# Queries, keys, the convolution's inputs and all gates as pairs of seven block products, with two of four weight sums made by accumulating transfers

## The chip, the cores and the metric

The kernel runs on one core of a Trainium2 chip. The metric is the device time of one execution in microseconds. TensorE multiplies matrices, VectorE and ScalarE work on tiles, GpSimd (POOL) and SyncE (SP) mostly issue transfers. Each engine runs its own instructions in the order in which they stand in the program and waits on semaphores for the others.

## What is computed

One step of a trunk with two layers, for 512 frames of a new stream (the prompt) and 8 x 16 frames of running streams (the sample), 640 rows together, in float32. All widths are multiples of 128; D_MODEL is 1024.

```python
for l in range(2):
    x = x + 0.5 * swiglu(rmsnorm(x), w_ffn1_gu[l], w_ffn1_down[l])
    h = rmsnorm(x)
    B, C, V, q, k, v, g = split(h @ w_in[l])        # 512 each, g: 2 x 1024
    g_conv, g_attn = split(sigmoid(g + b_gate[l]))
    y_conv = B * depthwise_conv3(C * V)             # new_conv: last two rows of C * V
    y_attn = softmax(q k^T / 8 + bias, banded) v    # 8 heads x 64; sample: cached keys, values
    m = g_conv * (y_conv @ w_conv_out[l]) + g_attn * (y_attn @ w_attn_out[l])
    x = x + m @ w_o[l]
    x = x + 0.5 * swiglu(rmsnorm(x), w_ffn2_gu[l], w_ffn2_down[l])
y = rmsnorm(x)                                      # also returned: k, v, new_conv of both layers
```

## The kernel before

**Layout and precision.** Everything is kept transposed: a tile has 128 features in its partitions and the 640 rows along it. Each float32 operand is split into a high and a low part (`whi`, `wlo` for weights, `hhi`, `hlo` for h), and a product is the sum of three matmuls: high with high, high with low, low with high. A projection to 128 columns is 8 tiles x 3 x 2 halves of 320 rows, 48 matmuls.

**Weights.** `wst` is one stream of slabs of 128 x 1024 in the order of use. `load` brings a slab into one of three `raw` buffers (issued by SP), `prep` casts it to its high part on ScalarE (L248), `flush` subtracts that for the low part on VectorE (L253). There are three buffers of each part; `slab` keeps two slabs prepared ahead of the one in use.

**Pairs by seven products.** The FFN's gate and up projections, and gates 4 to 15 of the mixer, are computed two at a time by seven products of half size instead of eight (a scheme of Strassen's kind). Their seven left factors are weight blocks and sums of weight blocks, their right factors halves of h and differences of such halves. `source` makes four weight sums for each pair on VectorE. One block product is 12 matmuls of 320 columns (`block`, L331). Three PSUM tiles pa, pb, pc take them in turn, and between the products parts are copied out by ScalarE (c1, u2, c5) and added by VectorE.

**A layer** is FFN, mixer, FFN. In the mixer the order on TensorE is: q and k of the first head pair, V for all rows (L1051), and then attention, with `fill(n)` between its steps; `fill` takes the next n steps (8 weight tiles make a projection's 8 steps of 6 matmuls each) of a stream of projections: q and k of the other head pairs, then for each of four column groups C, V and B of the convolution, then two gates. For each head pair p, `scores(p)` multiplies queries with keys for both heads (L1089; reductions with bias L1091), `softmax` takes exponentials on ScalarE (L1221) and scales on VectorE (L1225), `values(p)` transposes (L1111), copies (L1113) and multiplies with v (L1124). Then the eight sample streams follow: `sscores(b)` (L1160) and `svalues(b)` (L1175 to L1193). After that come gates 2 and 3, the first output products (`out`, 24 matmuls each), the pairs of gates with two output products each, and w_o.

**Who orders what.** In the FFNs and from gate 2 on TensorE, VectorE and ScalarE run in the order of the code. In the attention only TensorE's order is the code's; the framework's scheduler places the instructions of VectorE, ScalarE, POOL and SP.

**PSUM.** The eight banks are two double tiles `acc` (projections; scores of the widest tile) and four single tiles `att`. A projection alternates between the two `acc` tiles, and VectorE scales it out with the rows' norm `rr` (L422, L1012).

Of the kernel before, what the change touches and what calls it, by code (L numbers as in the profile page):

```python
# [10 lines left out]
F32 = mybir.dt.float32  # L11
# [32 lines left out]
GP = 4  # L44

# [35 lines left out]
def mixer_order():  # L81


    out = [("g", m) for m in range(GP)] + [("co", m) for m in range(GP)]
    for b, name in enumerate(("co", "ao")):
        for m in range(0 if b else GP, KT, 2):
            out += [("gu", b * KT + m), (name, m), (name, m + 1)]
    return out + [("o", m) for m in range(KT)]


def kinds():
# [23 lines left out]
    for l in range(L):  # L115
        ffn(f"a{l}")
        held = KT * (3 * CT + 3 * AW // P)
        for what, _ in mixer_order():
            if what == "gu":
                plain(held)  # L120
                held = 0
                out.append("mix")
            else:
                held += KT if what in ("g", "o") else CT
        plain(held)
        ffn(f"b{l}")
# [12 lines left out]
def trunk(ctx: ExitStack, tc: tile.TileContext, xin, wst, small, pbias, samplebias, kcache, vcache,  # L139
# [10 lines left out]
    ps2 = ctx.enter_context(tc.tile_pool(name="ps2", bufs=2, space=PSUM))  # L150
    ps1 = ctx.enter_context(tc.tile_pool(name="ps1", bufs=4, space=PSUM))
# [3 lines left out]
    def acc(name):  # L155
        return ps2.tile([P, 2, 512], F32, tag="acc", name=name)

    def att(name):
        return ps1.tile([P, 512], F32, tag="att", name=name)
# [21 lines left out]
    sums, pool = {}, [None]  # L181
# [16 lines left out]
    def source(i):  # L198
# [3 lines left out]
        if i not in sources:  # L202
# [4 lines left out]
            elif arg == 0:  # L207
                sources[i] = [(ra, whole)]
            else:
# [148 lines left out]
    def norm(name, goff, ssum):  # L358
# [21 lines left out]
        def sums():  # L380
            st.sums([ssum], att(f"nps{name}"))
            st.roots()
            st.turn(ssum, st.r)

        def spread():
            for a in range(2):
                c = slice(a * HT, (a + 1) * HT)
                ps = att(f"nbc{name}_{a}")[:, :HT]
# [254 lines left out]

    def gate_up(fp, n, ex, first, turned, tails, put, j):
# [160 lines left out]
    def mixer(l, after):  # L805
        with tc.tile_pool(name=f"yp{l}", bufs=1, reuse_waits="tile") as yp:
# [4 lines left out]
            ycs = [yp.tile([P, T], F32, name=f"yc{l}_{c}") for c in range(CT)]  # L811
            with tc.tile_pool(name=f"mp{l}", bufs=2, reuse_waits="tile") as mp:
                cn = mp.tile([P, CT, 2 * (1 + NB)], F32, name=f"cn{l}", bufs=1)
                gates = {}

                def gate(m, then=None):
                    for _ in gate_steps(m, then):
                        pass

                def gate_steps(m, then=None):  # L820
                    pg = acc(f"pgate{l}_{m}")
                    yield from steps(pg, h)
                    if then:
                        then()
                    gates[m] = tmp(f"g{l}_{m}")
                    scaled(gates[m], pg, rr)
                    sigmoid(gates[m], m)

                def sigmoid(g, m, scale=1.0):
                    bg = O_BG + l * 2 * KT + m  # L830
                    ACT.activation(g, g, AF.Sigmoid, bias=sm[:, bg : bg + 1], scale=scale)

                def others():
                    for c in range(CT):
                        yield from conv(l, c, h, rr, cn, ycs[c])
                    POOL.dma_start(co[l], cn)
                    for m in range(2):
                        yield from gate_steps(m)

                with tc.manual_schedule(engines={mybir.EngineType.PE}):  # L840
                    attention(l, h, st, stats, mp, yas, others())
            with tc.tile_pool(name=f"gp{l}", bufs=1, reuse_waits="tile") as gp, \
                 tc.manual_schedule(engines=ORDERED):
                hold[0] = True
                mo = outputs(l, gp, h, st, ycs, yas, gate, sigmoid, gates)
# [13 lines left out]
    def outputs(l, gp, h, st, ycs, yas, gate, sigmoid, gates):  # L859
# [6 lines left out]
        ts = [tuple(gp.tile([P, 4, HT], F32R, name=f"t{i}{l}_{kp}") for i in ("hi", "lo"))  # L866
              for kp in range(NP)]

        A, B = (0, 1), (2, 3)

        def operands(kp, two):

            z = spare[kp % 2].rearrange("p a (b t) -> p (a b) t", b=2)
            (xe, ge), (xo, go) = ((x[k], O_GM + l * KT + k) for k in (2 * kp, 2 * kp + 1))
            ge, no, go = sm[:, ge : ge + 1], less[:, go - O_GM : go - O_GM + 1], sm[:, go : go + 1]
            if two is A:
                ACT.activation(z[:, 3], xe[:, t2], AF.Copy, scale=ge)
            for o, a, s, b in (((1, xe[:, t1], ge, 3), (0, xo[:, t2], no, 1)) if two is A else
                               ((2, xo[:, t2], go, 3), (3, xo[:, t1], no, 0))):
                DVE.scalar_tensor_tensor(out=z[:, o], in0=a, scalar=s, in1=z[:, b],  # L880
                                         op0=ALU.mult, op1=ALU.subtract)
            c = slice(two[0], two[1] + 1)
            ACT.copy(ts[kp][0][:, c], z[:, c])

        def rest(kp, two):
            z = spare[kp % 2].rearrange("p a (b t) -> p (a b) t", b=2)
            c = slice(two[0], two[1] + 1)
            DVE.tensor_tensor(out=ts[kp][1][:, c], in0=z[:, c], in1=ts[kp][0][:, c].bitcast(F32),
                              op=ALU.subtract)

        def halves_of_h(odd, c):
            return lambda kp: tuple(z[:, c] for z in h[2 * kp + odd])

        def made(i):
            return lambda kp: tuple(z[:, i] for z in ts[kp])

        X11, X21, X22 = halves_of_h(0, t1), halves_of_h(1, t1), halves_of_h(1, t2)
        XN6, XT5, XT7, XT4 = (made(i) for i in range(4))
        c1, u2 = st.caps[:, t1], st.caps[:, t2]
        every = range(NP)  # L900

        def gate_pair(m, then=None):
# [3 lines left out]
            c5 = gp.tile([P, HT], F32, tag="cap", name=f"c5_{n}")  # L906
# [60 lines left out]
        gate(2, lambda: (flush(), take(yc, "yc", ycs), operands(0, A), operands(0, B)))  # L967
        flush()
        gate(3, lambda: (rest(0, A), rest(0, B), operands(1, A), operands(1, B)))
        rest(1, A)  # L970
        rest(1, B)
        operands(2, A)
        flush()
        out(0, yc)
        rest(2, A)
        operands(3, A)
        out(1, yc)
        rest(3, A)
        operands(2, B)
        out(2, yc)  # L980
        rest(2, B)
        operands(3, B)
        out(3, yc)
        rest(3, B)
        for m in range(GP, 2 * KT, 2):
# [8 lines left out]
    def attention(l, h, norms, stats, mp, yas, others):  # L994
# [13 lines left out]
        def qproj(p):  # L1008
            pq = acc(f"pq{l}_{p}")
            yield from steps(pq, h)  # L1010
            t = qa[p] = mp.tile([P, T], F32, name=f"q{l}_{p}", tag="q")
            DVE.scalar_tensor_tensor(out=halves(t), in0=two(pq), scalar=HD ** -0.5,  # L1012
# [493 lines left out]
```

## Time and profile before

| | |
|---|---|
| median of 3 runs | 2611.59 us (2611.41 to 2613.09) |
| profiled execution, its own time | 2611.54 us |
| its span | 2609.8 us |
| TensorE busy | 2591.7 us, 17864 matmul records |
| VectorE, ScalarE, POOL busy | 1831.2, 1053.3, 46.4 us |
| granted TensorE clock | full in every slice |
| HBM traffic | 90 GB/s over the span |

The page lists busy time by engine and groups of instructions by line. A matmul's record is about 0.31 us long for 320 columns, but records overlap, so that the time on the path is read from the chain of waits. PE is TensorE, DVE VectorE, ACT ScalarE. Times in the timeline and the chain are microseconds from the span's start.

### The profile page before, as it was taken

The numbers are of one execution on the slowest core, as the hardware profiler recorded it, in microseconds if no ns is written. First come the engines' busy times: TensorE is split into PE (matmuls) and PEld (weight loads), VectorE is DVE, ScalarE is ACT, GpSimd is POOL, SyncE is SP. The second block draws the span as 40 slices with busy tenths as digits, with TensorE's granted clock in tenths as the row PEclk, the third lists the DMA queues.
The fourth block names the chain that finished last, engine by engine and source line by source line (L and its number), as shares of the span: only waits on it lengthen the run. The fifth ranks groups of instructions, "written<-read, shape, count | busy, mean of one in ns | idle before, by whom it ended". The sixth has DMA issues, their size and how long they took to land.

```text
span 2609.8 us, 42561 instructions
## 1 busy us (share of the span) xinstructions
PE 2591.7 (99%) x17864; PEld 2538.0 (97%) x17864; DVE 1831.2 (70%) x2771; ACT 1053.3 (40%) x1586; POOL 46.4 (2%) x137
## 2 busy tenths in 40 slices
PE   8999999999999999999999999999999999999998
PEld 8999999889999999999999999998899999999998
DVE  7687767364777887767787667664547778867676
ACT  5343334342444443334454333343324445433332
POOL 0000000110000000000000000001100000000000
PEclk9999999999999999999999999999999999999999
DMA  3222223334222132222222222233331222222222
GB/s 131 73 105 82 73 89 116 110 104 140 67 81 89 59 112 82 73 89 81 82 81 98 75 92 77 86 116 113 112 132 65 81 81 75 90 93 75 88 90 74
DMA packets 73808, 237.06 MB, mean 91 GB/s; under 512 B 7984, under 2 KB 18864, under 8 KB 73616
## 3 DMA queue, kind: packets, MB, share of 16 engines
q1 hardware_dynamic: 70016, 223.90, 25.3%
q0 software_dynamic: 2880, 9.79, 1.0%
q8 instruction: 140, 2.29, 0.3%
q10 hardware_dynamic: 720, 0.65, 0.1%
q14 instruction: 52, 0.43, 0.1%
HBM read 225.85 MB, written 7.94 MB: 90 GB/s over the span
## 4 chain that ended last, share of the span: by engine, by line
PE 94%; DVE 4%; ACT 1%; issue 0%; DMA 0%; SPq 0%; DVEq 0%; ACTq 0%
PE pab L331 12%; PE pda L317 11%; PE pdb L317 11%; PE paa L331 11%; PE pcb L331 6%; PE pca L331 5%; PE py L317 4%; PE po L317 4%; PE qa L331 3%; PE pbb L331 3%; PE pba L331 3%; PE pc L317 2%; PE pq L317 2%; PE pb L317 2%; PE pgate L317 2%; PE pcv L317 2%
## 5 line engine op out<-in xcount | busy, mean ns | idle before, releaser
L253 DVE TENSOR_TENSOR wlo<-raw,whi 128x1024 fp32r<-128x1024 f32 (+2 forms) x492 | 530.4, 1083 | 177.1 <-ACT whi L248 177.1
L248 ACT CAST whi<-raw 128x1024 fp32r<-128x1024 f32 (+2 forms) x492 | 461.3, 940 | 349.8 <-PE pca L331 79.4
L331 PE MATMUL pab<-xhib,whi 128*128 128x320 f32 x704 | 218.4, 310 | 0.4 <-ACT u_b L728 0.4
L331 PE MATMUL pab<-xlob,whi 128*128 128x320 f32 x704 | 217.4, 309 | 0.0
L331 PE MATMUL pab<-xhib,wlo 128*128 128x320 f32 x704 | 217.4, 309 | 0.0
L331 PE MATMUL paa<-xhia,whi 128*128 128x320 f32 x640 | 198.2, 310 | 0.7 <-ACT c_a L664 0.5
L331 PE MATMUL paa<-xloa,whi 128*128 128x320 f32 x640 | 197.7, 309 | 0.0
L331 PE MATMUL paa<-xhia,wlo 128*128 128x320 f32 x640 | 197.7, 309 | 0.0
L317 PE MATMUL pda<-ahia,whi 128*128 128x320 f32 x704 | 160.4, 309 | 0.6 <-DVE x L794 0.6
L317 PE MATMUL pda<-aloa,whi 128*128 128x320 f32 x704 | 160.4, 309 | 0.0
L317 PE MATMUL pda<-ahia,wlo 128*128 128x320 f32 x704 | 160.4, 309 | 0.0
L317 PE MATMUL pdb<-alob,whi 128*128 128x320 f32 x656 | 149.5, 309 | 0.0
L317 PE MATMUL pdb<-ahib,wlo 128*128 128x320 f32 x656 | 149.4, 309 | 0.0
L317 PE MATMUL pdb<-ahib,whi 128*128 128x320 f32 x656 | 149.4, 309 | 0.0
L331 PEld LDWEIGHTS pab<-xhib,whi 128*128 128x128 f32 x704 | 132.2, 188 | 1.2 <-ACT u_b L728 0.9
L331 PEld LDWEIGHTS pab<-xlob,whi 128*128 128x128 f32 x704 | 132.2, 188 | 0.2
L331 PEld LDWEIGHTS pab<-xhib,wlo 128*128 128x128 f32 x704 | 132.2, 188 | 0.0
L331 PEld LDWEIGHTS paa<-xhia,whi 128*128 128x128 f32 x640 | 120.2, 188 | 1.3 <-ACT c_a L664 0.8
L331 PEld LDWEIGHTS paa<-xloa,whi 128*128 128x128 f32 x640 | 120.2, 188 | 0.1
L331 PEld LDWEIGHTS paa<-xhia,wlo 128*128 128x128 f32 x640 | 120.2, 188 | 0.0
L248 ACT CAST whi<-s 128x1024 fp32r<-128x1024 f32 (+1 forms) x96 | 94.3, 982 | 63.4 <-DVE s L192 51.9
L317 PEld LDWEIGHTS pda<-ahia,whi 128*128 128x128 f32 x704 | 117.6, 188 | 1.1 <-issue 1.1
(486 smaller groups left out, 6689.8 us busy)
## 6 DMA issues: line engine op xcount, KB each, us to landing
raw<-in_wst SPq DMA_DIRECT2D x384, 512.0 KB, 3.5
kc<-in_kcache SPq DMA_DIRECT2D x16, 512.0 KB, 4.3
vc<-in_vcache SPq DMA_DIRECT2D x16, 512.0 KB, 4.4
bias<-in_pbias POOLq DMA_DIRECT2D x16, 256.0 KB, 3.1
x<-in_xin SPq DMA_DIRECT2D x8, 320.0 KB, 5.2
out_ko<-k POOLq DMA_DIRECT2D x8, 320.0 KB, 2.5
out_vo<-v POOLq DMA_DIRECT2D x10, 256.0 KB, 2.6
out_yout<-x SPq DMA_DIRECT2D x8, 192.0 KB, 1.9
```

Source lines behind the costliest of these rows:

```text
L248: ACT.copy(hi[:, d], src[:, c])
L253: DVE.tensor_tensor(out=lo, in0=src, in1=hi.bitcast(F32), op=ALU.subtract)
L317: PE.matmul(ps[:, a, :HT], w, x[:, a * HT : (a + 1) * HT], start=k == 0 and j == 0, stop=k == n - 1 and j == 2)
L331: PE.matmul(ps, a, b, start=start and kp == 0 and j == 0, stop=stop and kp == NP - 1 and j == 2, skip_group_check=True)
```

## The change

The projections q, k, C, V and B (four each of 128 columns) and gates 0 to 3 are now made in pairs by `seven`: q with k of a head pair, C with V of a column group, two B, two gates. V (the values) is projected first; q and k of the first head pair follow it. The right factors (`Operands`) are made once, at the end of the FFN and during V, and serve the gates as well; one of them takes the place of a half of h after V has used it. `rr` is applied after the pair, for C times V as its square.

Of a pair's four weight sums VectorE makes two, and two are made by transfers issued on POOL that add slab halves from HBM onto the raw buffer. This holds for the mixer's pairs, also for gates 4 to 15; the FFN's keep their sums. The sum that stays apart lies in SBUF instead of PSUM.

PSUM is divided anew by `layout`: in the attention four single banks `pr` for the pairs and four `att`; elsewhere as before. The widest score tile now uses `att` too, and the order of score tiles is 0, 1, 3, 2. In SBUF the sample's keys use the buffers of q and k (two transfers of half size for each stream), its scores those of the transposed weights, its new values those of the bias, and the scratch for POOL's transfer descriptors is set to 2048.

The stream that `fill` takes has 140 steps instead of 160; the sample's `fill(6 + b % 2)` becomes `fill(4)`.

```diff
 def mixer_order():
-    out = [("g", m) for m in range(GP)] + [("co", m) for m in range(GP)]
...
+    mix = lambda *rows: ("mix", rows)
+    out = [("v", None)] + [mix(("q", p), ("k", p)) for p in range(AW // P)]
+    for c in range(0, CT, 2):
+        out += [mix(("C", c + i), ("V", c + i)) for i in range(2)] + [mix(("B", c), ("B", c + 1))]
+    gates = [mix(("g", m), ("g", m + 1)) for m in range(0, 2 * KT, 2)]
...
     def source(i):
...
             elif arg == 0:
                 sources[i] = [(ra, whole)]
+                if kind == "mix":
+                    rb = load(n + 1)
+                    POOL.dma_start(rb[:, h1], wst[n + 1][:, h2], accum_op=ALU.add)
...
                 elif arg == 1:
                     flush()
-                    st = sums[n] = att(f"s6_{n}")
-                    add(ra[:, h1], ra[:, h1], rb[:, h1])
-                    add(st, ra[:, h1], rb[:, h2])
-                    add(rb[:, h1], rb[:, h1], rb[:, h2])
+                    st = sums[n] = spool[0].tile([P, CH // 2], F32, tag="s6", name=f"s6_{n}", bufs=1)
+                    add(st, rb[:, h1], ra[:, h1])
+                    POOL.dma_start(ra[:, h1], wst[n + 1][:, h1], accum_op=ALU.add)
                     sources[i] = [(st, h1), (rb, h1)]
...
+    def seven(n, bank, X, c1, u2, c5, first, second, third, last):
+        pa, pb, pc = (bank(f"m{i}{n}")[:, :HT] for i in "abc")
+        def mul(ps, s, half, x, start):
+            for ks in (range(NP // 2), range(NP // 2, NP)):
+                block(ps, s, half, x, ks, start, True)
+                yield
+        s = chunk()
+        yield from mul(pa, s, 0, X["11"], True)
+        ACT.copy(c1, pa)
+        yield from mul(pb, s, 1, X["21"], True)
+        first(pb)
+        s = chunk()
+        yield from mul(pa, s, 0, X["N6"], False)
+        ACT.copy(u2, pa)
+        yield from mul(pc, s, 1, X["T5"], True)
+        ACT.copy(c5, pc)
+        s = chunk()
+        yield from mul(pa, s, 0, X["T7"], False)
+        second(pa)
+        yield from mul(pc, s, 1, X["22"], False)
+        third(pc)
+        s = chunk()
+        yield from mul(pa, s, 0, X["T4"], False)
+        last(pa)
...
     def mixer(l, after):
...
+                def upper(u):
+                    return lambda pb: add(u[:, t1], pb, cs[0]), lambda pc: add(u[:, t2], pc, cs[1])
+                def lower(g, scale=-1.0):
+                    def by(c, src):
+                        DVE.scalar_tensor_tensor(out=g[:, c], in0=src, scalar=scale, in1=rr[:, c],
+                                                 op0=ALU.mult, op1=ALU.mult)
+                    def second(pa):
+                        add(g[:, t2], pa, cs[2])
+                        by(t2, g[:, t2])
+                    return second, lambda pa: by(t1, pa)
...
-    def attention(l, h, norms, stats, mp, yas, others):
+    def attention(l, h, norms, stats, ops, mp, yas, both, others):
...
-            for i in (0, NQ - 1, *range(1, NQ - 1)):
+            for i in (0, 1, NQ - 1, *range(2, NQ - 1)):
                 w = (i + 1) * P
-                if i == NQ - 1:
-                    both = acc(f"pss{l}_{p}")
-                    pss = [both[:, e, :w] for e in range(2)]
-                else:
-                    pss = [att(f"pss{l}_{hh}_{i}")[:, :w] for hh in heads]
+                pss = [att(f"pss{l}_{hh}_{i}")[:, :w] for hh in heads]
...
-    def conv(l, c, h, rr, cn, y):
+    def conv(l, c, pair, upper, c5, rr2, cn, y):
...
+        def third(pc):
+            half(pc)
+            DVE.tensor_tensor(out=ct, in0=ct, in1=rr2, op=ALU.mult)
+            minus(u[:, 2 + HT : 2 + SEQ], y[:, HT:SEQ], ct[:, HT:SEQ])
+            minus(us[:, :, 2:], samp(y), samp(ct))
...
+        yield from pair(f"cv{c}", first, lambda pa: add(y[:, t2], pa, c5), third,
+                        lambda pa: minus(u[:, 2 : 2 + HT], pa, ct[:, t1]))
```

More of the change, by code (lines that the diff above doesn't have):

```diff
@@ L812, in mixer @@
+            layout(f"a{l}", 0)
             with tc.tile_pool(name=f"mp{l}", bufs=2, reuse_waits="tile") as mp:
                 cn = mp.tile([P, CT, 2 * (1 + NB)], F32, name=f"cn{l}", bufs=1)
[L814 to L827, printed above, removed]
@@ L865, in outputs @@
         mm = ycs + [spare[i // 2][:, i % 2] for i in range(CT)]
[L866 to L899, printed above, removed]
+        X11, X21, X22, XN6, XT5, XT7, XT4 = (X[i] for i in ("11", "21", "22", "N6", "T5", "T7", "T4"))
+        c1, u2, c5 = cs
         every = range(NP)
@@ L965, in give @@
                 mo.append(parts(hp, "h", f"m{l}_{m}", mm[m]))
[L967 to L985, printed above, removed]
+        gate_pair(2, lambda: take(yc, "yc", ycs))
+        for m in range(4):
+            out(m, yc)
+        for m in range(4, 2 * KT, 2):
             gate_pair(m, (lambda: take(ya, "ya", [yas[:, c, :] for c in range(CT)])) if m == KT else None)
@@ L1378, in trunk @@
     fp.close()
+    ps.close()
 def _cols(w):
```

257 lines of the change are left out of this document (163 added, 94 removed).

## The prediction

> **What bounds the kernel.** I read the page's busy line and its chain of waits first, then busy time by stage, then the chain in order of time inside the mixer.
>
> ```profile
> PE 2591.7 (99%) x17864; PEld 2538.0 (97%) x17864; DVE 1831.2 (70%) x2771; ACT 1053.3 (40%) x1586; POOL 46.4 (2%) x137
> ...
> PE 94%; DVE 4%; ACT 1%; issue 0%; DMA 0%; SPq 0%; DVEq 0%; ACTq 0%
> ```
>
> TensorE is busy for 99% of the span and carries 94% of the chain. Whatever takes matmuls away shortens the run, as long as nothing else becomes late. So the stages that change have to be read one by one.
>
> ```profile
> core 0: us, PE busy (x) PEld busy (x) DVE busy (x) ACT busy (x) POOL busy (x), PEclk, DMA share, GB/s
> 412.00:447.00 35.00, 35.00 (x241) 35.00 (x240) 25.41 (x30) 16.40 (x21) 1.56 (x5) 1.00 0.42 139
> 490.60:578.00 87.40, 87.40 (x611) 77.48 (x611) 52.42 (x151) 37.97 (x97) 12.67 (x33) 1.00 0.30 101
> 578.00:676.00 98.00, 98.00 (x846) 89.47 (x841) 41.38 (x85) 28.08 (x53) 4.04 (x19) 1.00 0.40 134
> 720.00:820.00 100.00, 100.00 (x683) 100.00 (x682) 72.25 (x104) 44.24 (x65) 0.00 (x0) 1.00 0.25 85
> ```
>
> Of these windows of layer 0, the first is the end of the FFN ahead of the mixer, the second the prompt attention (softmax of eight heads between projections), the third the sample attention, the fourth the gates. TensorE never stops in any of them. VectorE has 52.4 of 87.4 us in the prompt attention and 41.4 of 98 in the sample attention: room on average. The question is what each single wait then becomes.
>
> **The saving.** The chain gives the price of a projection and of a pair by seven block products.
>
> ```profile
> 500.23 7.04 PE pk L317 x48
> ...
> 515.29 2.36 PE pss L1089 x16
> ...
> 521.36 7.04 PE pk L317 x48
> ...
> 536.42 2.36 PE pss L1089 x16
> ...
> 717.62 7.04 PE py L317 x48
> 736.99 7.04 PE py L317 x48
> ```
>
> A projection of 48 matmuls takes 7.04 us on the path, or 0.147 us per matmul, although one record lasts 0.31 (they overlap). From 717.62 to 736.99 lie one gate pair by seven products and two output products of 24 matmuls (together 7.04): the pair costs 19.37 - 7.04 = 12.33, where two projections cost 14.08. The change makes pairs of four q with k, four C with V, two B and two of gates in each layer, 24 in all. They save 24 x 1.75 = **42.0 us**. The block products already run at this price, so nothing on TensorE itself can spoil it. Gates 4 to 15 were pairs before and keep their matmuls.
>
> **What becomes tight.** A projection had two double banks, and VectorE had 7 us to empty one. `seven` writes blocks of 12 matmuls, 1.76 us each, into three banks of a ring of four: pa, pb, pa, pc, pa, pc, pa. A bank must be read before the next block but one: three ScalarE copies (c1, u2 of pa, c5 of pc), VectorE's `second` (pa plus c5), and `last`, which frees pa for the next pair's pb. Each has 1.76 us of cover. The FFN, ordered by hand, does this with next to no wait:
>
> ```profile
> PE paa L331 <- ACT c_a L664: 0.5, 1, 0.5
> ```
>
> ```profile
> L192 DVE TENSOR_TENSOR ga<-paa,c_a x40: 484/491/493, 78.9 to 1697.2; 128x320 f32<-128x320 f32 x40
> L742 DVE TENSOR_TENSOR ga<-paa,rhoa x40: 482/484/492, 81.7 to 1700.6; 128x320 f32<-128x320 f32 x40
> L717 ACT COPY c_a<-paa x38: 406/425/428, 98.1 to 1690.1; 128x320 f32<-128x320 f32 x38
> ```
>
> An eviction needs 0.4 or 0.5 us. But in the attention only TensorE's order is written by hand; on ScalarE and VectorE the scheduler interleaves the evictions with softmax. In the order of the built program, the same in both layers, they stand behind it. The rows of before price that queue; next starts are taken from start to start.
>
> ```profile
> 515.84 0.29 DVE L1091 CUSTOM_DVE_ANT_0 s<-pss,bias 128x128 f32<-128x128 f32 x1 [4.39 <-issue]
> ...
> 517.24 0.69 DVE L1091 CUSTOM_DVE_ANT_0 s<-pss,bias 128x512 f32<-128x512 f32 x1
> ...
> 517.85 0.42 DVE L1091 CUSTOM_DVE_ANT_0 s<-pss,bias 128x256 f32<-128x256 f32 x1
> ...
> 518.54 0.55 DVE L1091 CUSTOM_DVE_ANT_0 s<-pss,bias 128x384 f32<-128x384 f32 x1
> ...
> 519.49 0.29 DVE L1219 TENSOR_SCALAR st<-st 128x4 f32<-128x4 f32 x2
> ...
> 522.17 0.79 DVE L1012 SCALAR_TENSOR_TENSOR q<-pq,rrm 128x640 f32<-128x640 f32 x1
> 522.88 1.34 DVE L1225 TENSOR_SCALAR s<-s,st 128x128 f32<-128x128 f32 x4
> ...
> 524.48 1.28 DVE L1225 TENSOR_SCALAR s<-s,st 128x128 f32<-128x128 f32 x4
> 525.67 1.22 DVE L253 TENSOR_TENSOR wlo<-raw,whi 128x1024 fp32r<-128x1024 f32 x1
> ```
>
> ```profile
> 519.75 0.40 ACT L1221 ACTIVATE s<-s,st 128x128 f32<-128x128 f32 x1 [3.81 <-DVE st L1219]
> ...
> 521.95 0.39 ACT L1221 ACTIVATE s<-s,st 128x128 f32<-128x128 f32 x1
> ...
> 524.14 1.03 ACT L248 CAST whi<-raw 128x1024 fp32r<-128x1024 f32 x1
> ```
>
> With scores at 515.3 as zero: reductions of the two heads' tiles from 0.6 to 4.2, eight exponentials from 4.4 to 8.8 (2.2 a head), each head's four scalings 1.3, the next weights' low part 1.2, high part 1.0. In the new kernel the reductions of the wide tile wait for nothing extra, but all eight score tiles share four banks, so the scores take 2.65 instead of 2.36: 0.3 each time. Then, period by period (zero at the scores' start):
>
> - Scores 0 come between blocks 2 and 3 of the second q,k pair. A half low part (0.6) sits among the reductions; exponentials run 4.3 to 8.7. The u2 copy is behind all eight, done at 9.15. TensorE has done blocks 3 and 4 at 2.65 + 3.52 = 6.17 and block 5 needs u2: 3.0. With the banks 3.3.
> - Scores 1 come after block 3. The c5 copy is behind the exponentials (3.75 to 8.15) and is ready at 8.6; TensorE stands from 6.17: 2.4. Then `second` is behind the second head's scalings (9.6) and a low part (10.8), done at 11.25, where block 6 ended at 10.36: 0.9. The next pair's first weight sum stands ahead of the reductions and waits for its transfer: 0.3 (below). With the banks 3.9.
> - Scores 2 come after block 4. A weight sum among the reductions costs 0.3 more on the banks. `last` stands behind a q eviction and both heads' scalings (11.2), a half low part and itself: 12.2; the next pair's pb wants it at 10.0. In all 2.9.
> - Scores 3 come after block 5. `last` is behind one head's scalings: 0.8. c1 of the next pair is behind the exponentials, three casts and the convolution's first tap: 1.15. With the banks 2.25.
>
> That is 12.35 a layer, **+24.7 us**. Bounds: 6 a layer, if short operations overlap more than their starts show; 17, if nine further evictions around them each meet half a cast (0.5).
>
> **Transfers.** Of a pair's four weight sums VectorE keeps two; two become accumulating transfers of 256 KB on the POOL queue, 72 in all. No accumulate is in the trace. Nearest rows:
>
> ```profile
> raw<-in_wst SPq DMA_DIRECT2D x384, 512.0 KB, 3.5
> ...
> bias<-in_pbias POOLq DMA_DIRECT2D x16, 256.0 KB, 3.1
> ```
>
> ```profile
> 519.39 1.06 POOL L1075 DMA_DIRECT2D bias<-in_pbias  x2 [10.08 <-DVE st L1091]
> ```
>
> A plain load of the same size on the same queue lands in 3.1 us, and issuing takes POOL 0.53. Below that I see no reason to go; twice it, 6.2, is the upper bound. I take 4.0, nearer the load, since reading the destination adds to the data and not to the fixed part. The Trainium skill (Collectives: The Full Stack, "The bandwidth ceiling: the fold count and why AG ≠ RS ≠ AR") says that an adding transfer is slowed by its two source reads, not by the addition. With the fit that the Trainium skill gives (DMA: Bandwidth & Descriptors, "Anatomy of one DMA — SWDGE (gpsimd) path") for twice the bytes, that is an estimate of 3.2 us; the sum by it would be 2592. No run here shows it yet.
>
> With three raw buffers the next pair's second half can be loaded only when this pair's third weight slab has been split, some 1.3 to 3 us into the pair. Add 3.5 and 4.0, and the sum can be made 9 to 11 us into the pair. The sample attention's order puts that add ahead of `second`. What the sample matmuls add there lengthens a pair:
>
> ```profile
> 585.04 0.38 PE L1175 MATMUL sptp<-ident,ss 128*128 128x128 f32 x2
> ...
> 588.10 0.67 PE L1160 MATMUL spss<-kc,bd 128*32 128x272 f32 x8
> 588.69 0.42 PE L1187 MATMUL spy<-vn,spn 16*32 16x128 f32 x8
> 589.04 0.65 PE L1187 MATMUL spy<-vc,spt 128*32 128x128 f32 x16
> ```
>
> about 2 us for each sample, nine half blocks of 0.88: a pair of fourteen lasts 15.4, and block 7 wants `second` at about 12.5. After the add come a low part and `second`, 2.1 us. In the first B pair the load is behind the sample's keys and the maximum's negation is behind the add; the exponential and c5 follow it, which costs 1.5. The other pairs come out within 0.5 and make 1.0. That is 2.5 a layer, **+5.0 us**; at 3.1 it would be about 1 for both layers, at 6.2 about 27 with what it adds in the prompt part. Each us of latency past 4.0 costs about 5 a layer. In front of the transfers POOL holds only issues, small copies and fills whose producers are done earlier; SP's loads wait for the sample's key buffers, which come free before the raw buffers do.
>
> In the gates the queue is ordered and a period is 19.37: the load starts 4.5 in, has landed and accumulated at 12.0, and the first sum is asked for at 13.9. Nothing; VectorE sheds two sums of four.
>
> **The rest.** V goes first, and the operands of the products (16 half-width tiles a layer) move from the gates into the FFN's end and V. VectorE has 25.4 of 35 us there, the change adds about 6 inside 3.5 us of slack per product: 0.5 a layer, between 0 and 2. Cover for V's evictions is the ending product. **+1.0 us**.
>
> Sum against the profiled execution's 2611.5 (span 2609.8 and 1.7 around it; the median is 2611.6): 2611.5 - 42.0 + 24.7 + 5.0 + 1.0 = **2600**. Bounds: -42 + 12 + 1 to -42 + 34 + 27 + 4, so 2582 to 2634.
>
> **Rivals.**
> *All hidden.* The FFN's pairs speak for it, VectorE's average too. Then only banks and a few tenths stay: 2575. The written order behind the exponentials speaks against it. 0.10.
> *The gain is just eaten.* If those nine evictions do meet half a cast each and the sample pairs lose 3.5 instead of 2.5, waits are 17 + 3.5 a layer, 41: 2611. 0.16.
> *Late accumulates.* They land after 6.2 us instead of 4.0. VectorE, which runs in order, stands at the add; `second`, c5 and through them blocks 6 and 7 wait in every sample pair and the scores of period 1 start their softmax late. 2600 + 2.2 x 10 = 2622, slower; it decides from about 5.2 us on. For it: the destination must be read too, and loads of keys run beside. Against: DMA engines are busy 0.40 at most. 0.22. The Trainium skill (SBUF — State Buffer, "SBUF: two separate sides" and the section on the bandwidth-pool intuition after it) has a rule of this kind: while VectorE is in a two-port mode, POOL cannot write descriptors, and a transfer of 0.62 us took 3.1. By that rule each transfer would take another 2.5 us, an estimate, and the time would be 2625. The trace does not bear it out: VectorE's scalings take 1.34 us for 1280 elements, no faster per element than its subtractions (1.22 for 1024), and POOL's two bias issues beside the reductions took their usual 1.06. It holds 0.03 of the 0.22.
> That the pairs don't save what they should is excluded by the 12.33 above.
>
> **Numbers.** The forecast near 2600 has 0.52. A measurement of this kernel tells about 0.2%, 5.2 us, from no change. Faster: 0.52 and 0.10, **0.62**; within: **0.16**; slower: **0.22**. The range leaves out 0.08 below and 0.12 above: 2586 to 2619, whose upper part is the late accumulates' shorter half. The likeliest case alone is 2590 to 2606.
>
> **What would show it.** Seven-block pairs of 12.33 without waits; TensorE waiting on the u2 copy in period 0, on c5 and `second` in period 1, on `last` in 2 and 3, about 3, 3, 2 and 2 us, twice; accumulates landing in about 4 us; no wait in the gates. TensorE's idle time should rise from 18 us to near 48. Wrong if TensorE waits for weight slabs (high or low parts), if accumulates take over 5 us, or if the scores' banks cost more than 0.5 a time.

## The result, and the profile after

The changed kernel takes 2657.76 us (median of 4 runs, 2655.37 to 2662.21) against 2611.81 (4 runs of the kernel before, 2611.41 to 2613.09): 1.0176 times as long, 95% interval 1.0160 to 1.0192. The forecast was 2600, its range ended at 2619, and the case "slower" had 0.22. The profiled execution took 2655.37 us, with a span of 2653.6.

The busy line and the accumulates' row of the DMA issues of the page after:

```profile
PE 2580.9 (97%) x17576; PEld 2513.8 (95%) x17576; DVE 1912.3 (72%) x2965; ACT 1117.7 (42%) x1738; POOL 119.2 (4%) x225
...
raw<-in_wst POOLq DMA_DIRECT2D x72, 256.0 KB, 4.1
```

The matmuls went as planned (17864 to 17576 records, 288 less: 24 pairs by 12). But TensorE's busy time fell by 10.8 us and not by 42, and its idle time (span less busy) rose from 18.1 to 72.7. So there are two losses to find: 54.6 us of new waits, and 31 us of busy time that should have gone and did not. Busy time by stage of layer 0 says where (V and the first pair; prompt attention; sample attention; gates from 4 on):

```profile
core 0: us, PE busy (x) PEld busy (x) DVE busy (x) ACT busy (x) POOL busy (x), PEclk, DMA share, GB/s
447.79:493.23 45.44, 45.44 (x244) 40.16 (x242) 28.61 (x44) 21.21 (x34) 8.04 (x13) 1.00 0.41 110
493.23:599.54 106.31, 92.78 (x593) 79.06 (x592) 72.25 (x191) 50.35 (x124) 21.61 (x42) 0.97 0.42 115
599.54:700.93 101.39, 85.26 (x722) 74.86 (x720) 61.87 (x134) 42.12 (x85) 15.80 (x34) 0.97 0.56 151
...
743.20:843.20 100.00, 99.51 (x678) 99.25 (x678) 66.31 (x94) 44.07 (x66) 7.87 (x9) 1.00 0.41 109
```

Only the two attention stages lose: 13.5 of 106 us and 16.1 of 101 us idle, and there alone the granted clock is below one (0.97). The gates have no loss worth the name. From the mixer's first product (a q before, a V now) to the first output product a layer took 243.8 us before and takes 265.6 (layer 0) and 264.6 (layer 1) now, although half of the expected saving, 21 us, lies in each. What TensorE waited for, the view of waits:

```profile
PE pss L1185 <- DVE st L1187: 13.5, 8, 2.8
PE mc_b L350 <- ACT c L682: 8.5, 2, 6.2
PE ma_cv L350 <- DVE yc L208: 6.3, 4, 2.0
...
PE qa L350 <- ACT ya L1299: 4.4, 2, 2.2
PE ma_b L350 <- ACT capsm L675: 4.3, 2, 2.3
PE mc_qk L350 <- ACT c L682: 3.5, 2, 1.9
PE ma_qk L350 <- ACT capsm L680: 3.5, 2, 2.5
PE ma_cv L350 <- ACT capsm L675: 3.4, 2, 1.7
PE spy L1289 <- DVE ss L1282: 3.1, 2, 1.6
PE ma_b L350 <- DVE sst L1320: 2.6, 2, 2.0
```

(Total us, times, longest.) The first row is the scores' banks, 13.5 us; the rows of the q,k pairs and c1 (`ma_cv` from L675) are the evictions behind softmax; the rest belongs to the sample stage, some 29 us. VectorE's own waits name what is behind them, first in the kernel before, then in the one after:

```profile
DVE s L192 <- DMA raw<-in_wst: 1.2, 4, 0.4
```

```profile
DVE s L208 <- DMA raw<-in_wst: 107.9, 38, 6.5
```

The first sum of a pair's weight blocks waited 1.2 us in all for its transfer; now VectorE stands at it for 107.9 us. What that does is seen at the worst wait, in the timelines of VectorE, ScalarE and TensorE in the first B pair:

```profile
613.96 0.08 DVE L1265 DVE_READ_ACCUMULATOR2_ANT sst<- 128x1 f32 x1
620.56 0.69 DVE L208 TENSOR_TENSOR s<-raw,raw 128x512 f32<-128x512 f32 x1 [6.52 <-DMA raw<-in_wst]
621.17 0.15 DVE L1320 TENSOR_SCALAR sst<-sst 128x1 f32<-128x1 f32 x1
...
621.41 0.52 ACT L1322 ACTIVATE ss<-ss,sst 128x272 f32<-128x272 f32 x1 [5.99 <-DVE sst L1320]
...
621.93 0.40 ACT L682 COPY c<-mc_b 128x320 f32<-128x320 f32 x1
...
622.38 0.63 PE L350 MATMUL mc_b<-hhim,whi 128*128 128x320 f32 x1 [6.20 <-ACT c L682]
```

VectorE has the sample's maximum at 614.0, but the sum of the next pair's weights stands ahead of its negation and waits until 620.56 for the accumulate. ScalarE's exponential waits for that negation, the copy c5 for the exponential, and TensorE for the copy: 6.2 us, for weights that no matmul needs yet. The chain of waits shows the same in layer 1 as a loop:

```profile
1959.72 3.55 DMA raw<-in_wst
...
1964.03 6.50 DMA raw<-in_wst
...
1971.32 1.12 DVE wlo L272
...
1979.35 3.41 DMA raw<-in_wst
...
1983.37 5.84 DMA raw<-in_wst
...
1989.23 0.70 DVE s L208
```

Load of a pair's second slab, accumulate into it, sum, and with the low part a buffer comes free for the next load: from 1959.72 to 1979.35 one round takes 19.6 us. The five rounds between 1902 and 1998 take 18.5 to 19.7 each. Four pairs of this stage (1913.9 to 1993.6) take 19.9 us each, where the same four take 15.9 in the kernel below that makes all sums on VectorE; the prediction had put 15.4.

### The profile page after: what moved, and what is told of

Read it like the earlier page. It is cut to its first block, busy times and chain, and to the rows that moved or that the text cites. A ratio compares the mean times of both kernels' runs of the same rounds, so it can differ in the third digit from the quotient of the medians.

```text
span 2653.6 us, 42700 instructions
## 1 busy us (share of the span) xinstructions
PE 2580.9 (97%) x17576; PEld 2513.8 (95%) x17576; DVE 1912.3 (72%) x2965; ACT 1117.7 (42%) x1738; POOL 119.2 (4%) x225
## 5 line engine op out<-in xcount | busy, mean ns | idle before, releaser
L272 DVE TENSOR_TENSOR wlo<-raw,whi 128x1024 fp32r<-128x1024 f32 (+2 forms) x540 | 563.0, 1047 | 183.6 <-ACT whi L267 183.1
L267 ACT CAST whi<-raw 128x1024 fp32r<-128x1024 f32 (+2 forms) x540 | 490.2, 912 | 298.1 <-PE pca L350 79.4
L267 ACT CAST whi<-s 128x1024 fp32r<-128x1024 f32 (+1 forms) x120 | 109.4, 912 | 123.0 <-DVE s L208 95.3
L272 DVE TENSOR_TENSOR wlo<-s,whi 128x1024 fp32r<-128x1024 f32 (+1 forms) x120 | 127.2, 1060 | 4.2 <-ACT whi L267 4.0
```

Of the source, the lines that this page charges most:

```text
L267: ACT.copy(hi[:, d], src[:, c])
L272: DVE.tensor_tensor(out=lo, in0=src, in1=hi.bitcast(F32), op=ALU.subtract)
```

## The experiments

Theory: late sums. VectorE stands at a weight sum (or at a low part whose high part waits) until an accumulate has landed, and reductions, negated maxima and evictions stand behind it. First rival: the queue that the prediction priced, evictions behind softmax. Second: weights are late by their loads alone.

One run of one version says little below 7 us: the four runs of the changed kernel lie between 2655.37 and 2662.21.

**Without the transfers, and with all sums on VectorE.** The first kernel leaves two of the four sums out, the second makes all four on VectorE.

```diff
-                    POOL.dma_start(rb[:, h1], wst[n + 1][:, h2], accum_op=ALU.add)
...
-                    add(st, rb[:, h1], ra[:, h1])
-                    POOL.dma_start(ra[:, h1], wst[n + 1][:, h1], accum_op=ALU.add)
+                    add(ra[:, h1], ra[:, h1], rb[:, h1])      # second kernel only; the first
+                    add(st, ra[:, h1], rb[:, h2])             # keeps add(st, rb, ra) alone
+                    add(rb[:, h1], rb[:, h1], rb[:, h2])
```

> The changed kernel without its 72 accumulating transfers: the two weight sums they make are left out (the slabs are used as loaded), everything else stays, the order of TensorE and all but 16 places of ScalarE's order included. Late sums (theory): VectorE runs in order and stands at a weight sum, or at a low part whose high part waits, until an accumulate of 4 to 7 us has landed; score reductions, negated maxima and evictions queue behind it. Then the 55 us of TensorE waits fall below 25, the clock losses behind them with them, and the time falls by 35 to 55 us: 2600 to 2622. Queue (the prediction's reason): evictions stand behind the softmax whatever the sums do; waits stay above 45 us, the time falls by less than 15: above 2640. Late loads: with three raw buffers the second slab of a pair is loaded late whether something is accumulated into it or not; only the accumulate's own 4 us per pair goes: 2625 to 2640.

> The changed kernel with all four weight sums of each mixer pair on VectorE (36 pairs, two more half-slab additions of 0.69 us each, 50 us of VectorE time), no accumulating transfers; result unchanged. Late sums: gains what the run without accumulates gains, less what the two additions of 1.4 us per pair cost where VectorE is late (5 to 15 us): 2608 to 2635, below 2640 in any case. Queue: VectorE gets longer, so evictions get later; no faster than the changed kernel, 2655 to 2680. Late loads: about 2635 to 2650.

Measured: 2599.99 without the accumulates, 2599.49 with four sums on VectorE (one run each, 2612.12 for the kernel before beside them). 58 us come back in both: the first time lies at the lower end of what the theory asked, the second below all three cases (the two additions cost nothing that shows, where 5 to 15 us had been allowed for). Both rivals are out as the main cause. VectorE is busy for 44 us longer in the second than in the changed kernel. The second kernel's busy line and TensorE's waits:

```profile
PE 2562.6 (99%) x17576; PEld 2504.6 (96%) x17576; DVE 1956.0 (75%) x3037; ACT 1118.3 (43%) x1738; POOL 61.5 (2%) x153
```

```profile
PE mc_qk L350 <- ACT c L682: 4.6, 2, 2.3
PE ma_qk L350 <- ACT capsm L680: 4.6, 2, 2.3
PE ma_cv L350 <- ACT capsm L675: 3.8, 4, 1.7
PE spy L1289 <- DVE ss L1282: 2.4, 2, 1.2
PE ma_qk L350 <- DVE k L208: 1.5, 2, 0.7
...
PE pss L1185 <- DVE st L1187: 0.4, 2, 0.2
```

The scores' banks (13.5 to 0.4) and nearly all of the sample stage's waits are gone. What stays is what the prediction named: c5, u2, c1 and `second` in the prompt periods.

**A plain transfer instead of an adding one.** `accum_op=ALU.add` is dropped in both places, so that the half slab is overwritten; the order on every engine stays as it is.

> The changed kernel with the order of all engines kept, only the 72 transfers overwrite the half slab instead of adding to it (the weight sums are wrong thereby). Price of adding: if the addition in the transfer is what makes the sums late (4.1 us against 3.1 for a plain load of the size, and 6 to 7 us beside the key loads), each us is worth what the prediction's rival said, about 5 a layer, and the time falls by 10 us or more: below 2648. Place in the chain: it is that a second transfer follows the load and VectorE stands at the sum behind it, adding or not; then a plain transfer lands within 0.5 us of an adding one and the time stays within 6 us of 2657.

Measured: 2620.45. Adding is worth 37 us, a plain transfer in the same place still 20.5 (against 2599.99 without). Both theories hold a part, and the price per us was too low in the first. The rows of POOL's issue, plain and then adding, and the plain landing:

```profile
L228 POOL DMA_DIRECT2D raw<-in_wst x36: 536/536/547, 456.4 to 2091.7; - x36
...
raw<-in_wst POOLq DMA_DIRECT2D x72, 256.0 KB, 3.1
```

```profile
L228 POOL DMA_DIRECT2D raw<-in_wst x36: 866/875/929, 457.5 to 2127.1; - x36
```

An adding transfer lands in 4.1 us against 3.1, and takes 0.88 us to issue against 0.54. Of the 36 that follow a load (L228) the medians are 4.7 and 3.4. So 1.0 to 1.3 us in each transfer make 37 us. The row of the adding ones behind a load:

```profile
DMA to landing us min/median/max: 3.9/4.7/7.3
```

**One transfer of the two.** First the one into the first slab is kept, then the one into the second:

```diff
-                    POOL.dma_start(rb[:, h1], wst[n + 1][:, h2], accum_op=ALU.add)   # first kernel
...
                     add(st, rb[:, h1], ra[:, h1])
+                    add(st, st, rb[:, h2])
+                    add(rb[:, h1], rb[:, h1], rb[:, h2])
                     POOL.dma_start(ra[:, h1], wst[n + 1][:, h1], accum_op=ALU.add)
# second kernel: the accumulate into rb kept, and
-                    POOL.dma_start(ra[:, h1], wst[n + 1][:, h1], accum_op=ALU.add)
+                    DVE.tensor_tensor(out=ra[:, h1], in0=st, in1=rb[:, h2], op=ALU.subtract)
```

> One of the two accumulating transfers kept: the one into the first slab of a pair, which is issued when that slab has been split and which only the high part of the pair's third weight slab waits for. The other sum is on VectorE, which has the four additions it has without any transfers. If the late sum into the second slab (load, then accumulate, then VectorE's add) is what costs: close to the run without accumulates, 2600 to 2612. If either transfer costs alike: about half of the 58 us come back, 2622 to 2636.

> The other one kept: the accumulate into the second slab right behind its load, which VectorE's first sum waits for; the first slab's sum is a subtraction on VectorE. If the late sum costs: most of the loss stays, 2635 to 2655. If either transfer costs alike: 2622 to 2636.

Measured: 2602.91 and 2667.13 (the second is above both expectations). VectorE's wait at the first sum and TensorE's for the scores' banks, in the one and in the other:

```profile
DVE s L208 <- DMA raw<-in_wst: 19.9, 22, 1.8
...
PE pss L1186 <- DVE st L1188: 0.4, 1, 0.4
```

```profile
DVE s L208 <- DMA raw<-in_wst: 114.3, 38, 6.7
...
PE pss L1185 <- DVE st L1187: 12.0, 7, 2.2
```

The transfer into the first slab is nearly free; the one that follows a load and that VectorE's sum waits for has the whole loss, and more. The 36 that are left in the second kernel land in 4.9 us by the median. It is 9 us slower than the kernel with both. Of the 11.7 us between the two profiled spans 4.5 are idle time; the rest is busy time, and its TensorE clock was at half for 61 us in all against 34 (more on this below). Why its waits cost more clock is open; its order on VectorE is not quite the same.

**Order by hand.** All sums on VectorE, and in the attention VectorE's and ScalarE's order written out, with one softmax step per half block:

```diff
+        PLAN = ("e0", "e0", "e0", "e0", "e1 r0", "e1 s0", "e1 s0", "e1 s0", "s0", "r1 s1", "s1 s1", "s1")
...
+            for step in PLAN:
+                for op in step.split():
+                    todo[int(op[1])][op[0]].pop(0)()
+                fill(1)
```

> All four sums on VectorE, and in the attention VectorE's and ScalarE's order written by hand too: each eviction right behind its block, one exponential or scaling of the softmax per half block between them, the sample's reduction and softmax behind its transposes, low parts one slab later. TensorE's order is unchanged. Queue: the 17 us of waits that stay without accumulates (u2 2.3, c5 2.3, second 0.7, c1 1.7, sample 1.2 a layer) are evictions behind softmax; put between them they go, with their clock losses and restarts (6 us): 2572 to 2588. Capacity: VectorE, busy for 18 of 21 us of a prompt period, and ScalarE are too full for any order; waits move but stay, 2592 to 2612.

Measured: 2693.04, worse than either expectation. u2 and c5 wait no more, but in this order the high parts stand ahead of the evictions on ScalarE and wait for sums that stand behind the convolution on VectorE; `ma_cv` and `ma_b` waited 41 us for the copies of c1 behind them. This tells of that order, not of the engines' capacity, as the next runs show.

**Evictions first.** The scheduler keeps the order, but evictions get a higher priority, without and with the transfers:

```diff
-        ACT.copy(u2, pa)
+        with tc.high_priority():
+            ACT.copy(u2, pa)
```

and so for c1, c5, `first`, `second`, `third`, `last`.

> All four sums on VectorE as before, and the evictions of the pairs (c1, u2, c5 on ScalarE; the four additions and scalings on VectorE) given a higher priority in the scheduler, so that in the built order they stand ahead of softmax steps that the scheduler still has waiting: u2 and c5 of the first prompt period behind one and two exponentials instead of eight, c5 of the second behind four. TensorE's order is unchanged. Queue: of the 17 us of waits that stay without transfers, the 4.6 for u2, about half of the 4.6 for c5 and some of c1's go, each with half as much again in clock and restarts: 2586 to 2594. If those waits are not made by the order but by ScalarE's and VectorE's load, they only move: 2597 to 2606.

> The changed kernel with its accumulating transfers, and only the evictions' priority raised. Late sums: the waits behind the sums stay (score reductions, sample softmax), only the evictions' share of about 12 us can shrink: 2643 to 2656. Queue (the prediction's main term): order is what costs, and most of the loss goes: below 2625.

Measured: 2596.29 (4 runs, 2594.12 to 2599.0; 0.9944 of before, 0.9928 to 0.9961), and 2655.52 with the transfers. The second settles the rival: with late sums the evictions' order is worth 2 us, which is nothing beside the spread of 7. The first lies between its two cases (2586 to 2594, 2597 to 2606): the evictions' waits are gone, and one new row stands in their place:

```profile
PE ma_qk L350 <- DVE wlo L272: 9.9, 4, 2.6
```

**Evictions and weight parts first.** The same for the casts of `prep` and the subtractions of `flush` in the attention:

```diff
-            ACT.copy(hi[:, d], src[:, c])
+            with urgent():                 # tc.high_priority() inside the attention
+                ACT.copy(hi[:, d], src[:, c])
```

> As the run with the evictions first, and the weights' high and low parts of the attention raised too. With the evictions alone their waits of 11.9 us went and 9.9 us of waits for low parts came (four of 2.3 to 2.6, in the first two prompt periods, where the high part stood behind all eight exponentials and the low part behind the scalings). Queue: with both ahead of the softmax, which is wanted only 10.6 us after the scores, these go too, and 14 us with their restarts: 2580 to 2587. Capacity: ScalarE and VectorE are too full in a prompt period; the softmax then comes late and the transposes wait: 2592 to 2602.

Measured: 2592.81 (5 runs, 2591.39 to 2593.65; 0.9926, 0.9913 to 0.9940). The low parts' waits are gone; idle time is 25.3 us, 7 above the kernel before. But the gain is 3.5 us, where the queue's case asked for 9 to 16; the time lies in the case called capacity. The waits that came in place of the others are those of the transposes, which now come before their scalings, and some for the scores' banks (1.7):

```profile
PE ptp L1221 <- DVE s L1341: 2.4, 4, 0.7
```

**Fewer key loads beside the accumulates.** Back to the changed kernel:

```diff
-            kcs = []
-            for e, tag in enumerate("qk"):
+            kcs = old[b - 2][0] if b > 1 else []
+            for e, tag in enumerate("qk" if b < 2 else ""):
```

and the same for the values.

> The changed kernel, transfers included, in which samples 2 to 7 of each layer read the cached keys and values of samples 0 and 1 instead of loading their own (36 loads of 256 and 512 KB less in all, on SP's queue; their attention is of the wrong cache thereby). The order on TensorE, VectorE, ScalarE and GpSimd is unchanged. Crowding: in the sample stage the accumulates (6 to 7 us in places) and the weight loads are late because key and value loads run beside them and stand ahead of them on SP's queue; then accumulates land in 4 to 4.5 us there, the 23 us of waits of the sample stages halve, and the time falls by 12 to 25 us: 2632 to 2646. Loop: each pair's slab waits for one accumulate, its split frees the buffer, the next load and the next accumulate follow, some 15 us or more with nothing beside them; then the waits stay above 17 us and the time falls by less than 9: above 2648.

In this kernel samples 2 to 7 read the keys and values of samples 0 and 1. Measured: 2646.71, 11 us less, between the two expectations: the worst wait fell from 6.2 to 3.3 us, VectorE's wait at the sums only from 107.9 to 101.9, and the transfers behind a load land in 4.6 us instead of 4.7. Crowding by the sample's loads is a part, about a fifth of the 58; the rest of the loss is there without them.

**Scores in two parts, and transposes later.** Both from the kernel with evictions and weight parts first:

```diff
             for i in (0, 1, NQ - 1, *range(2, NQ - 1)):
+                if i == NQ - 1:
+                    fill(1)                # first kernel; fill(11) follows
# second kernel
-            fill(12)
+            fill(13)
...
-            fill(2)                        # ahead of the value products
+            fill(1)
```

> As the run with evictions and splits first, and one half block of the twelve that follow each period's scores is moved between their fourth and fifth tile (the only change in TensorE's order). The scores took 12.5 us a layer there against 9.4 before, as eight tiles share four banks and VectorE must read four before the next. Banks: the half block covers that wait, 0.6 us for each of eight periods: 2586 to 2590. VectorE's chain: the reductions end when they end, and the transposes wait for the scalings by as much more: 2590 to 2596.

> As the run with evictions and splits first, and in each prompt period 13 half blocks instead of 12 between the scores and the transposes, 1 instead of 2 ahead of the value products. In that run the transposes waited for the scalings (2.4 us) and their copies, and took 10.6 us a layer against 8.1 before. Softmax late: one half block more, 0.88 us, covers most of it, 3 to 4 us a layer: 2584 to 2589. Otherwise the wait moves to the value products, which get one half block less: 2590 to 2595.

Measured: 2594.75 (0.9935, 0.9921 to 0.9948) and 2587.73 (4 runs, 2587.07 to 2588.0; 0.9906, 0.9889 to 0.9922). The first came out in its second case, VectorE's chain: the banks' waits of 1.7 us went, and those of the transposes grew from 3.8 to 5.0, with small new ones beside them. The second did what was expected. It is the fastest version, some 25 us faster than the kernel before (2612.39 beside it), with all of the block products and an idle time of 23.4 us.

One experiment is missing: no run keeps both transfers and lets VectorE take the sum later, behind the operations that now queue behind it. That the sum holds them up is read from the timelines and from the two runs with one transfer each.

## Why the prediction was wrong

**The saving (42.0).** Right as a price: in the gates a pair takes 2069.74 - 2057.41 = 12.33 us, as forecast:

```profile
2057.41 1.76 PE qa L350 x12
...
2069.74 5.28 PE py L336 x36
```

"Nothing on TensorE itself can spoil it" was wrong. Giving each matmul in TensorE's timeline the time to the next start, less waits, the projections of both layers took 347.5 us before and the blocks 321.3 after: 26.2 less and not 42. The scores took 30.3 against 19.0. With 2.9 for the rest and 54.6 of waits this is 42.6 of the span's 43.8 us. Part of this is the clock, next. Part is the scores themselves: in the kernel with all sums on VectorE, where almost no wait for banks is left and no score stands at a lowered clock, they still take 25.0 us, 0.75 more each time than before, where the banks were to cost 0.3.

**The clock (no term).** Here is a step that was missing altogether. Three waits for an example: 2.56 us for the scores' banks, to 496.72; 2.52 us for u2, to 504.94; 6.20 us for c5, to 622.38. The windows around them:

```profile
core 0: us, PE busy (x), PEclk, DMA share, GB/s
491.75:495.16 3.41, 2.41 (x19) 1.00 0.60 156
495.16:498.58 3.42, 1.86 (x8) 1.00 0.39 129
...
501.99:505.40 3.41, 0.89 (x6) 1.00 0.81 219
505.40:508.82 3.42, 3.42 (x15) 0.50 0.00 0
...
618.04:621.46 3.42, 0.00 (x0) 1.00 0.57 146
621.46:624.87 3.41, 2.48 (x10) 0.50 0.10 11
624.87:628.28 3.41, 3.41 (x15) 0.50 0.38 65
```

These windows are not chosen freely. In the traces of all 14 kernels every change of the granted clock lies a whole number of 3.413 us behind the first one, and the rows are windows of that grid. The second wait fills most of one window, and the next window has half the clock. The first, no shorter, falls across two windows, each still busy for more than half, and costs no clock. The third empties a window, and two windows at half clock follow. Counted over the 14 traces, from 30 to 2570 us and by the profile's records: of the windows at full clock in which TensorE was busy for less than 0.45, all 56 were followed by one at half clock; from 0.45 to 0.65 it was 11 of 83; above 0.65 none of 10191. The Trainium skill (TensorE: Matmul & The Clock Gate, "Part 1: The HAM clock gate (the "warmup" mystery)") says that the clock is halved after an idle window of about 3.4 us and comes back after as long a busy one. The half and the length agree; that the window must be idle does not, since 0.89 us of work in it (501.99) did not prevent the half.

The changed kernel has eight such stretches inside its layers, of one or two windows, 34 us in all, and TensorE was busy for 33 of them. Half of that, 16 us, is an estimate of what they cost: about half of the 31. The price of a wait in clock varies much: by the same estimate the kernel with all sums on VectorE lost 3 us with 17.0 of new idle time, the one with evictions first none with 14.1, and the one with the second slab's transfer alone 27 with 59.1.

**Prompt waits (24.7).** Nearly right in sum, wrong in kind. The evictions behind softmax were forecast at 21.7 us with what the banks do not take: u2 6.0, c5 4.8, `second` 1.8, `last` 6.2, c1 2.3 and 0.6 for the first sum. After they measure 11.7 (u2 3.5, c5 3.5, `second` 1.3, c1 3.4, `last` none), without transfers 14.5 (4.6, 4.6, 1.5, 3.8). The mechanism was right, `last` was costed too high. The banks were forecast at 0.3 a time and measured 13.5 us in eight times, past the 0.5 that the prediction set as its own refutation. VectorE and ScalarE in the first period show why:

```profile
493.75 1.04 ACT L267 CAST whi<-raw 128x1024 fp32r<-128x1024 f32 x1 [3.57 <-PE pss L1185]
...
494.83 1.23 DVE L272 TENSOR_TENSOR wlo<-raw,whi 128x1024 fp32r<-128x1024 f32 x1 [2.01 <-ACT whi L267]
```

The low part of the third slab stands ahead of the score reductions on VectorE, its high part waits 3.57 us, and what that reads is the buffer into which an accumulate was issued at 489.60. (The profile names the scores, which feed nothing here; without transfers the same cast waits 0.6 us and the banks not at all.) That accumulate is late because the sum ahead of it was: it is issued behind VectorE's sum at 488.24, which had waited for the transfer into the second slab. With the first slab's transfer alone its counterpart is issued at 486.42, and the banks wait 0.4 us in the whole run; with the second slab's alone they wait 12.0. "The reductions of the wide tile wait for nothing extra" held for the order and not for what that order waits on.

**Accumulating transfers (5.0).** The term that failed most. The latency was right: 4.0 taken, 4.1 measured by the median. The Trainium skill's fit (DMA: Bandwidth & Descriptors, "Anatomy of one DMA — SWDGE (gpsimd) path") for twice the bytes had given an estimate of 3.2; a plain transfer took 3.1, the adding one 4.1, so the measurement decides against that estimate. (Nor did it go with 2592: by the prediction's own price, about 1 at 3.1 us instead of 5.0, the sum would have been 2596.) Wrong was what was built on the latency. First, the median hides the transfers that matter: those behind a load landed in 4.7 us by the median and in up to 7.3 (4.9 in the kernel with these alone). Second, the load behind which they go was to start 1.3 to 3 us into a pair, since "this pair's third weight slab" was to be split by then. That slab itself takes an accumulate, which the working did not follow: in the first B pair (from 602.46) its high part starts at 606.79, the load at 609.12, 6.7 us into the pair, and the sum at 620.56, 18 us into the pair and not 9 to 11. Loads, adding transfers and splits thus make a loop of 19.6 us round against pairs of 15.9. Third, "each us past 4.0 costs about 5 a layer" was linear below a loop that was already the longest: the 1.0 to 1.3 us between plain and adding transfers cost 37 us, some 14 to 19 a layer for each. The sample stage's waits came to 29 us instead of 5.0. The rival "late accumulates" had the right mechanism (VectorE in order at the add, `second`, c5 and the softmax behind it), but put its start at 5.2 us and its price at 2622. Its rule for 0.03 of it, that POOL's descriptors wait for VectorE, is not borne out: POOL's 72 issues took 0.866 to 0.929 us, whatever VectorE did beside them. (The reading given against it was loose: 1.34 us for 1280 elements is 1.05 ns each, 1.22 for 1024 is 1.19, so the scalings were a little faster.)

**The rest (1.0) and the gates (nothing).** Right for TensorE: no wait at V, none of weight in the gates, where a period is 19.37 us. The timing behind it was not: in the first gate pair after the outputs begin (from 727.5) the accumulate has landed at 745.1, 17.6 us in and not 12.0, and VectorE stands at sums in the gates for 26 of its 107.9 us. It costs nothing there because TensorE needs none of what queues behind the sum so soon.

Without the transfers the time is 2599.5, next to the forecast of 2600. That is chance as much as merit: new waits were 17 us there instead of the 30.7 forecast, and 13 us went to matmuls that took longer (the scores alone 6, the clock some 3), for which the sum had next to nothing.

## What to carry to other kernels

On an engine that runs in order, an operation that waits for a transfer costs everything queued behind it, however much spare time the engine has: before work is moved from such an engine to a transfer, follow the whole loop (which split frees the buffer for which load, which transfer comes behind it, which instruction waits) and compare its round with the work's period, not one latency with one slack. The 44 us of VectorE's time that the transfers saved were worth nothing beside its waits for them at the head of its queue, some 81 us in the attention. When TensorE is the bound, new waits can cost up to nearly half as much again in clock; how much depends on whether they empty most of a window of 3.41 us.

## What the runs showed of the hardware that was not expected

An accumulating transfer of 256 KB from HBM costs GpSimd 0.88 us to issue against 0.54 for a plain one, and lands in 4.1 us against 3.1 by the median; behind a load it is 4.7 against 3.4. TensorE's clock changed on a fixed grid of 3.413 us: a window in which TensorE was busy for less than 0.45 was followed by one at half clock in all 56 cases, so that a wait of 2.52 us cost clock and one of 2.56 us, lying across two windows, did not. The changed kernel was at half clock for 34 us with 54.6 us of new idle time, the hand-written order for 61 us with 82.6, the kernel with evictions first not at all with 14.1.
